# An mLSTM recurrence laid beside projection matmuls: TensorE's order left to a scheduler, or written out as one visit per chunk

## The chip, the core and the metric

The kernel runs on one core of a Trainium2 chip. The metric is the device time of one execution in microseconds (us), and smaller is better. The engines that matter here work in parallel, each through its own list of instructions in a fixed order: PE (TensorE, matmuls and transposes), DVE (VectorE), ACT (ScalarE), POOL (GpSimd) and SP (which issues most DMAs). An engine waits at an instruction whose input isn't there yet, and all that stands behind it on that engine waits too.

## What is computed

The program is one inference step of a two-layer encoder with width 1024, over 1024 prompt rows and 32 rows of a second sequence (1056 in all). Layer 0 mixes the rows by an mLSTM with 4 heads; then come an MLP, a layer with band attention, and another MLP. The change lies in layer 0. Cut to what matters there:

```python
def mlstm_mixer(u, conv_prev, C0, n0, m0, w_in, b_if, conv_w, conv_b, mhn_g, w_out, chunk_len):
    proj = u @ w_in                      # q,k | v | o | gates
    ...
    qk, conv_new = causal_conv(qk_pre, conv_prev, conv_w, conv_b)
    qk = jax.nn.silu(qk)
    ...
    h, C, n, m = mlstm_scan(q, k, vh, ig, lf, C0, n0, m0, chunk_len)
    mu = h.mean(-1, keepdims=True)
    var = jnp.square(h - mu).mean(-1, keepdims=True)
    h = (h - mu) * lax.rsqrt(var + HEAD_NORM_EPS) * mhn_g
    h = h.reshape(Bsz, S, V_A) * jax.nn.sigmoid(o_pre)
    return h @ w_out, conv_new, C, n, m

def mlstm_chunk(carry, xs):              # one chunk of the scan, for each head
    ...
    s = jnp.einsum('bthd,bshd->btsh', q, k) * wts
    num = jnp.einsum('btsh,bshv->bthv', s, v) + a[..., None] * jnp.einsum('bhvd,bthd->bthv', C, q)
    den = s.sum(axis=2) + a * jnp.einsum('bhd,bthd->bth', n, q)
    h = num / jnp.maximum(jnp.abs(den), jnp.exp(-m_t))[..., None]
    ...
    C_new = a_last[..., None, None] * C + jnp.einsum('bsh,bshv,bshd->bhvd', w_s, v, k)
```

The outputs also hold the final states C of each head for both sequences.

## The kernel before, in words

**Projections.** All matrices are multiplied as three matmuls of split operands (high by high, high by low, low by high): `proj` at L118 to L120 for the projections q and k (`qk`, 128 output rows by 384 or 288 columns) and the output gate (`o`), and `v_chunk` at L487 to L489 for v. One group is 24 matmuls into one PSUM tile. The groups of one head are `qk_proj` (two times three column blocks), then `v_proj` (nine row blocks); `o_proj([0, 1])` comes after the last head.

**The recurrence.** The generator `mlstm(h, ...)` walks over the 9 chunks of head h (8 of 128 rows, and the 32 rows of the second sequence). In visit i it does, for chunk i, `scores` (TensorE: the scores `S` at L668, and a transpose of k at L669; DVE multiplies by the weights into `sT`, L671; ACT scales k into `kw`, L677; POOL makes `qc`, L675); for chunk i-1, `values` (TensorE: the numerator `num` at L686 and L688, the state update `cu` at L690; DVE: the new state `ct` at L693 and statistics `st` at L705; ACT copies the numerator into `hn`, L708); for chunk i-2, `state_out` (only chunks 7 and 8: transposes `co`, and a DMA). After every third chunk `scales` runs a chain of small steps on `sm`, 128 by 3 (L715 to L727, DVE but for two steps on ACT), and then ACT normalises the three `hn` (L731). `heads` transposes the normalised chunk (`hT`, L738) and ACT copies it to `G` (L739). `S`, `hT`, the transposed state `clp` (L660, chunk 8) and `co` share two PSUM buffers (the tag `tp`); `num` and `cu` share two others, and the projections have three.

**What sets the order.** `Flow` holds generators, and `flow.tick()` advances each. While head h projects, the recurrence of head h-1 is advanced by one visit after each projection group. A second task, `ada_l0`, is advanced by the same ticks. It computes the conditioning vectors of later stages on DVE: 128 by 512 multiply-adds (L281 and L279, `ada_acc`), transposes and sums (L288, L290), and a few tiny matmuls (`adas`). The calls only give the order in which instructions are written. A scheduler then builds the list of each engine from a priority heap and a cost model, unless an engine is named in `tc.manual_schedule`, where the written order stays. Before the change that is not so here, and the scheduler places the recurrence's matmuls one by one among the projection's.

Of the kernel before, what the change touches and what calls it, by code (L numbers as in the profile page):

```python
# [8 lines left out]
F32 = mybir.dt.float32  # L9
# [6 lines left out]
P = 128  # L16
# [5 lines left out]
NT = T // P + 1  # L22
# [4 lines left out]
NH = 4  # L27
# [48 lines left out]
def trunk_kernel(ctx: ExitStack, tc: tile.TileContext, a, o):  # L76
    nc = tc.nc
    flow = Flow()
# [94 lines left out]
    def mmt(name):  # L173
        return pa.tile([P, 512], F32, tag="mm", name=name, bufs=3)
# [197 lines left out]
    def uap(hl, k, t0, n):  # L372
        off = hl * UF + k * T + t0
        return U[:, off:off + n]
# [12 lines left out]
    A = A_cm.__enter__()  # L387
# [85 lines left out]
    def v_weight(h, half):  # L473
        def srcs(raw):
            r0 = 512 * half
            r = [(raw[:, :, 0:256],
                  w_in[r0:r0 + 512, 1024 + h * 256:1024 + (h + 1) * 256].rearrange("(k p) c -> p k c", p=P))]
            if h == 0:
                r.append((raw[:, :, 256:264], w_in[r0:r0 + 512, 3072:3080].rearrange("(k p) c -> p k c", p=P)))
            return r  # L480
        return wtile(f"v{h}_{half}", srcs, 264 if h == 0 else 256)

    def v_chunk(ps, ws, t, k):
        w = ws[k // 4]
        n = w.shape[-1]
        uh, ul = uap(0, k, t * P, P), uap(1, k, t * P, P)
        nc.tensor.matmul(ps[:, :n], uh, w[:, 0, k % 4, :], start=(k == 0), stop=False)  # L487
        nc.tensor.matmul(ps[:, :n], uh, w[:, 1, k % 4, :], start=False, stop=False)
        nc.tensor.matmul(ps[:, :n], ul, w[:, 0, k % 4, :], start=False, stop=(k == KC - 1))  # L489

    def v_out(ps, h, t):
        m = P if t < NT - 1 else TS
        vt = A.tile([P, 258], F32, tag="vt", name=f"vt_{h}_{t}", bufs=9)
        nc.scalar.copy(vt[:m, :256], ps[:m, :256])
        nc.gpsimd.memset(vt[:m, 256:258], 1.0)
        if h == 0:
            nc.vector.tensor_copy(bass.AP(g64.tensor, g64[:m, t, 0:4].offset, [g64[:m].ap[0], [32, 2], [1, 4]]),
                                  ps[:m, 256:264].rearrange("p (a b) -> p a b", a=2))
        return vt

    def v_proj(h, after):
        ws = [v_weight(h, half) for half in range(2)]
        vts = []
        for t in range(NT):
            ps = mmt(f"v_{h}_{t}")
            for k in range(KC):
                v_chunk(ps, ws, t, k)
            vts.append(v_out(ps, h, t))
            after(t)
        return vts  # L510
# [72 lines left out]
    def qk_proj(h, after):  # L583
        def srcs(r0):
            return lambda raw: [(raw[:, :, j * P:(j + 1) * P],
                                 w_in[r0:r0 + 512, j * 512 + h * P:j * 512 + (h + 1) * P].rearrange(
                                     "(k p) c -> p k c", p=P)) for j in range(2)]
        ws = [wtile(f"qk{h}_{i}", srcs(512 * i)) for i in range(2)]
        out = []
        for j in range(2):  # L590
            f = j * 4 + h
            qkp = (y4_tile if (h, j) == (0, 1) else y_tile)([P, YL], f"qkp_{f}")
            nc.gpsimd.memset(qkp[:, 0:3], 0.0)
            nc.gpsimd.tensor_copy(qkp[:, TP + 3:TP + 6], hist[:, f])
            for t0, n in TBS:
                ps = mmt(f"qk_{f}_{t0}")
                proj(ps[:, :n], n, ws, j, lambda hl, k: uap(hl, k, t0, n))
                for off, m, cnd in segs(t0, n):
                    d = t0 + off + 3 + 3 * cnd
                    nc.scalar.copy(qkp[:, d:d + m], ps[:, off:off + m])  # L600
                if TBS[-1][0] == t0:
                    continue
                after()
            nc.gpsimd.tensor_copy(tails[:, 0:3, f], qkp[:, TP:TP + 3])
            nc.gpsimd.tensor_copy(tails[:, 3:6, f], qkp[:, YL - 3:YL])
            y = A.tile([P, YL], F32, tag="y", name=f"y_{f}", bufs=4)
            N = YL - 3
            nc.vector.tensor_scalar(y[:, :N], qkp[:, 0:N], convw[:, f:f + 1], convb[:, f:f + 1],
                                    op0=ALU.mult, op1=ALU.add)
            for i in range(1, 4):  # L610
                nc.vector.scalar_tensor_tensor(y[:, :N], qkp[:, i:i + N], convw[:, i * 8 + f:i * 8 + f + 1], y[:, :N],
                                               op0=ALU.mult, op1=ALU.add)
            for s0, s1 in ((0, 353), (353, 706), (706, N)):
                tmp = A.tile([P, 384], F32, tag="tmp", name=f"sl_{f}_{s0}", bufs=3)[:, :s1 - s0]
                neglogsig(tmp, y[:, s0:s1])
                nc.scalar.activation(tmp, tmp, AF.Exp)
                nc.vector.scalar_tensor_tensor(y[:, s0:s1], y[:, s0:s1], float(P) ** -0.5 if j == 0 else 1.0, tmp,
                                               op0=ALU.mult, op1=ALU.mult)
            out.append(y)
            after()  # L620
        return out

    def o_proj(hs, after):

        ws = {h: [wblock(f"o{h}_{i}", w_in, 512 * i, 2048 + h * 256) for i in range(2)] for h in hs}
        for t0, n in TBS:
            for h in hs:
                for j in range(2):
                    f = 2 * h + j
                    ps = mmt(f"o_{f}_{t0}")  # L630
                    proj(ps[:, :n], n, ws[h], j, lambda hl, k: uap(hl, k, t0, n))
                    tmp = A.tile([P, 384], F32, tag="tmp", name=f"og_{f}_{t0}", bufs=3)[:, :n]
                    neglogsig(tmp, ps[:, :n])
                    nc.scalar.activation(tmp, tmp, AF.Exp)
                    g = G[:, f, t0:t0 + n]
                    nc.vector.scalar_tensor_tensor(g, g, mhg[:, f:f + 1], tmp, op0=ALU.mult, op1=ALU.mult)
                    after()

    def mlstm(h, qT, kT, vts):
# [93 lines left out]
        def heads(c):  # L733
            L, yo, to = geo(c)
            hn = live.pop(c)
            pth = tpt(f"hT_{h}_{c}")
            for j in range(2):
                nc.tensor.transpose(pth[:, j * P:j * P + L], hn[:L, j * P:(j + 1) * P], ident[:L, :L])  # L738
            nc.scalar.copy(G[:, 2 * h:2 * h + 2, to:to + L], pth[:, :256].rearrange("p (j t) -> p j t", j=2)[:, :, :L])  # L739

        def state_out(c):
            if c >= NCK - 1:
                w = 0 if c == NCK - 1 else 1
                nc.gpsimd.tensor_copy(ncol[:, 4 * w + h:4 * w + h + 1], ct[c][:, 256:257])
                ps = tpt(f"co_{h}_{c}")
                for j in range(2):
                    nc.tensor.transpose(ps[:, j * P:(j + 1) * P], ct[c][:, j * P:(j + 1) * P], ident)
                co = A.tile([P, 256], F32, tag="hn", name=f"co_{h}_{c}", bufs=4)
                nc.scalar.copy(co, ps[:, :256])
                nc.sync.dma_start(o["C_s" if w else "C_p"][0, 0, h].rearrange("(j p) k -> p j k", p=P),  # L750
                                  co.rearrange("p (j k) -> p j k", j=2))

        for i in range(NT + 3):
            if i < NT:
                scores(i)
            if 1 <= i <= NT:
                values(i - 1)
            if 2 <= i < NT + 2:
                state_out(i - 2)
            if i >= 4 and i % 3:  # L760
                for c in (i - 4, i - 3)[:3 - i % 3] if i % 3 == 1 else (i - 3,):
                    heads(c)
            yield

    def tick(*_):
# [36 lines left out]
    vts = [v_first(vw, next_u)]  # L802
# [19 lines left out]
    qk = [qk_proj(0, tick)]  # L822
    flow.finish(gates)
    G = A.tile([P, KC, T], F32, tag="G", name="G")
    ml = None
    for h in range(1, NH):
        unit = [0]

        def after_qk():
            unit[0] += 1  # L830
            if h > 1 or unit[0] >= 3:
                flow.tick()
        if h == 1:
            ml = flow.add(mlstm(0, *qk[0], vts[0]))
        qk.append(qk_proj(h, after_qk))
        vts.append(v_proj(h, tick))
        flow.finish(ml)
        ml = flow.add(mlstm(h, *qk[h], vts[h]))
    o_proj([0, 1], tick)
    flow.finish(ml)  # L840

    def out_rows():
        ps = tpt("tails_ps")
# [740 lines left out]
    mm, norm, _, out_proj, _, add_gated_at = make_layer(acc, bank, uap)  # L1584
# [333 lines left out]
    for gp in range(2):  # L1918
        for i in range(17):
            c = slim[gp][i // 2] if i % 2 else wide[i // 2] if i < 16 else slim[gp][8]  # L1920
            if not gp and i < 2:
                c = 7 + i
# [244 lines left out]
```

## Time and profile before

| what | value |
|---|---|
| median of 3 runs | 2411.29 us (2409.8 to 2412.41) |
| profiled execution, its own time | 2412.41 us |
| its span in the profile | 2410.6 us |
| TensorE busy | 2342.7 us, 97% of the span |
| DVE busy | 1939.0 us, 80% |
| ACT busy | 1206.0 us, 50% |
| mean granted TensorE clock | 0.995 of full speed |

The changed part runs from about 98 us (the projections of the second head, with the recurrence of the first beside it) to about 386 us (the recurrence of the last head beside the output gates). Times in the trace count from the start of the span. The share of busy time is an average over all stages; for the change, the rows of this part decide.

### The profile page before, as it was taken

The page shows a single profiled execution, that of the slowest core. Times are in us where ns is not written, and L with a number is a line of the kernel's source. Part 1 is how long each engine was busy: PE and PEld are TensorE (multiplying, and loading weights), DVE is VectorE, ACT ScalarE, POOL GpSimd, SP SyncE. Part 2 cuts the span into 40 slices and gives each one's busy share as a digit, 9 for nine tenths or more (in the row PEclk, how much of TensorE's full clock was granted, in tenths as well). Part 3 has the DMA queues.
Part 4 walks back from the last instruction along what each step waited for, and adds up shares of the span by engine and source line. Part 5 has one row for each costly group of instructions (what it writes and reads, how often), then busy time and mean ns, then how long its engine had stood idle before and what let it go on. Part 6 is the DMA issues. An engine that isn't in the chain of part 4 may idle for free. (4 is left out here: it accounts for less than half of the span.)

```text
span 2410.6 us, 44188 instructions
## 1 busy us (share of the span) xinstructions
PE 2342.7 (97%) x17180; PEld 2250.4 (93%) x17180; DVE 1939.0 (80%) x3903; ACT 1206.0 (50%) x2454; POOL 168.1 (7%) x320
## 2 busy tenths in 40 slices
PE   7999999999999999999999999999999999899997
PEld 4999999999999999999999987789999999899997
DVE  4888766778788789989888777756998889888778
ACT  4565557278666630101147467773776777222212
POOL 0111100000000000000000224420000000000003
PEclk9999999999999999999999999999999999999999
DMA  8343222526566896675512330051486779976642
GB/s 302 120 131 103 78 89 66 177 91 206 184 198 200 279 336 230 252 261 215 183 56 89 82 93 1 10 140 59 165 278 211 259 278 335 355 256 236 224 146 73
DMA packets 284277, 424.64 MB, mean 176 GB/s; under 512 B 15384, under 2 KB 205228, under 8 KB 278948
## 3 DMA queue, kind: packets, MB, share of 16 engines
q1 hardware_dynamic: 279860, 391.48, 48.3%
q10 hardware_dynamic: 4208, 30.35, 3.1%
q8 instruction: 135, 2.21, 0.4%
q14 instruction: 74, 0.61, 0.1%
HBM read 305.96 MB, written 118.17 MB: 176 GB/s over the span
## 5 line engine op out<-in xcount | busy, mean ns | idle before, releaser
L1082 DVE SCALAR_TENSOR_TENSOR ACX<-dn,ada,ACX 128x264 f32<-128x264 f32 (+6 forms) x664 | 281.8, 447 | 83.2 <-PE dn L1452 41.1
L1452 PE MATMUL dn<-fx,wf_d 128*128 128x264 f32 x2016 | 254.1, 285 | 6.8 <-DVE ACX L1082 3.5
L1452 PEld LDWEIGHTS dn<-fx,wf_d 128*128 128x128 f32 x2016 | 248.8, 188 | 9.0 <-DVE ACX L1082 3.0
L89 ACT CAST w_dn<-raw_dn 128x1024 fp32r<-128x1024 f32 x36 | 37.7, 1050 | 282.1 <-DVE aw L279 136.9
L118 PE MATMUL dn<-hs,w_dn 128*128 128x384 f32 (+2 forms) x512 | 161.2, 315 | 0.0
L119 PE MATMUL dn<-hs,w_dn 128*128 128x384 f32 (+2 forms) x512 | 161.0, 315 | 0.0
L120 PE MATMUL dn<-hs,w_dn 128*128 128x384 f32 (+2 forms) x512 | 156.4, 314 | 1.3 <-DVE w_dn L90 1.3
L1317 PE MATMUL up<-TF,wf_u 128*128 128x264 f32 x1056 | 143.2, 285 | 3.8 <-ACT H L1320 3.8
L1317 PE MATMUL up<-U,wf_u 128*128 128x264 f32 x1056 | 140.3, 285 | 1.7 <-ACT H L1320 1.2
L1317 PE MATMUL up<-u,wf_u 128*128 128x264 f32 x1056 | 139.7, 285 | 1.3 <-ACT wf_u L89 0.7
L279 DVE SCALAR_TENSOR_TENSOR aw<-radw,cs,aw 128x512 f32<-128x512 f32 x196 | 139.5, 743 | 1.1 <-DMA radw<-in_w_ada_dram 1.1
L1317 PEld LDWEIGHTS up<-TF,wf_u 128*128 128x128 f32 x1056 | 134.4, 189 | 4.8 <-ACT H L1320 4.6
L1317 PEld LDWEIGHTS up<-U,wf_u 128*128 128x128 f32 x1056 | 133.0, 188 | 3.0 <-ACT H L1320 1.6
L1317 PEld LDWEIGHTS up<-u,wf_u 128*128 128x128 f32 x1056 | 132.9, 188 | 1.9 <-ACT wf_u L89 0.9
L118 PE MATMUL dn<-U,w_dn 128*128 128x384 f32 (+2 forms) x416 | 129.4, 312 | 0.6 <-DVE ada L304 0.6
L119 PE MATMUL dn<-U,w_dn 128*128 128x384 f32 (+2 forms) x416 | 129.4, 312 | 0.0
L120 PE MATMUL dn<-U,w_dn 128*128 128x384 f32 (+2 forms) x416 | 125.9, 313 | 0.6 <-DVE w_dn L90 0.5
L1817 ACT ACTIVATE p<-p,mx 128x576 f32<-128x576 f32 (+9 forms) x132 | 86.6, 657 | 27.5 <-DVE mx L1814 25.2
L120 PEld LDWEIGHTS dn<-hs,w_dn 128*128 128x128 f32 x512 | 96.0, 188 | 2.0 <-DVE w_dn L90 1.8
L118 PEld LDWEIGHTS dn<-hs,w_dn 128*128 128x128 f32 x512 | 96.5, 189 | 0.1
L119 PEld LDWEIGHTS dn<-hs,w_dn 128*128 128x128 f32 x512 | 96.6, 189 | 0.0
L90 DVE TENSOR_TENSOR HL<-H,HL 128x1056 fp32r<-128x1056 f32 x64 | 80.3, 1254 | 20.0 <-ACT HL L89 19.9
(403 smaller groups left out, 7111.0 us busy)
## 6 DMA issues: line engine op xcount, KB each, us to landing
hpl<-HL SPq DMA_DIRECT2D x144, 264.0 KB
rdn_u<-in_w_up_dram SPq DMA_DIRECT2D x64, 512.0 KB
hd<-HL SPq DMA_DIRECT2D x28, 1056.0 KB
fx<-hd SPq DMA_DIRECT2D x50, 528.0 KB
radw<-in_w_ada_dram SPq DMA_DIRECT2D x24, 1024.0 KB
hd<-HM SPq DMA_DIRECT2D x28, 792.0 KB
raw_up<-in_w_up_dram SPq DMA_DIRECT2D x40, 512.0 KB
raw_dn<-in_w_down_dram SPq DMA_DIRECT2D x36, 512.0 KB
```

The costliest lines, as they stand in the source:

```text
L89: nc.scalar.copy(dst_h, src)
L90: (eng or nc.vector).tensor_sub(dst_l, src, dst_h.bitcast(F32))
L118: nc.tensor.matmul(ps, wh, mov(0, k), start=(k == 0), stop=False)
L119: nc.tensor.matmul(ps, wh, mov(1, k), start=False, stop=False)
L120: nc.tensor.matmul(ps, wl, mov(0, k), start=False, stop=(k == nk - 1))
L279: nc.vector.scalar_tensor_tensor(acc[cnd], raw[:, k], sc, acc[cnd], op0=ALU.mult, op1=ALU.add)
L1082: nc.vector.scalar_tensor_tensor(xs, ps[:, off + o:off + o + mm_], gate[:, fc, cnd:cnd + 1], xs, op0=ALU.mult, op1=ALU.add)
L1317: nc.tensor.matmul(p, self.ws[w][:, wl, k], moving(f, tp, xl, k), start=first and k + n_ == 0, stop=k == 3 and n_ == 2, skip_group_check=n ...
L1452: nc.tensor.matmul(p, ws[w][:, wl, k], t[:, s0, xl], start=first and k + n_ == 0, stop=k == kg - 1 and n_ == 2, skip_group_check=not first)
L1817: nc.scalar.activation(z, z, AF.Exp, bias=mx[:, 0:1], scale=-1.0, accum_out=mx[:, 1:2])
```

## The change

Three edits. The loop over the heads 2 to 4, and `o_proj([0, 1])` with the rest of the recurrence, stand in `tc.manual_schedule` for PE, so TensorE's list there is the written order: one whole projection group, one visit, the next group. In a visit the order is now `heads`, `state_out`, `scores`, `values` (before: `scores`, `values`, `state_out`, `heads`), and `heads` comes one visit later: chunks 0 and 1 in visit 5, 2 in visit 6, 3 and 4 in visit 8, 5 in visit 9, 6 and 7 in visit 11, 8 in visit 12. The tile `co` leaves the four `hn` buffers for the three `tmp` buffers. The lists of the other engines stay with the scheduler.

```diff
-                co = A.tile([P, 256], F32, tag="hn", name=f"co_{h}_{c}", bufs=4)
+                co = A.tile([P, 384], F32, tag="tmp", name=f"co_{h}_{c}", bufs=3)[:, :256]
...
-        for i in range(NT + 3):
+        for i in range(NT + 4):
+            if i >= 5 and i % 3 != 1:
+                for c in (i - 5, i - 4) if i % 3 == 2 else (i - 4,):
+                    heads(c)
+            if 2 <= i < NT + 2:
+                state_out(i - 2)
             if i < NT:
                 scores(i)
             if 1 <= i <= NT:
                 values(i - 1)
-            if 2 <= i < NT + 2:
-                state_out(i - 2)
-            if i >= 4 and i % 3:
-                for c in (i - 4, i - 3)[:3 - i % 3] if i % 3 == 1 else (i - 3,):
-                    heads(c)
             yield
...
-    for h in range(1, NH):
+    with tc.manual_schedule(engines={mybir.EngineType.PE}):
+        for h in range(1, NH):
...
-    o_proj([0, 1], tick)
+        o_proj([0, 1], tick)
         flow.finish(ml)
```

On TensorE, visit 5 of the first head, before. The names are a tile's name, the chunk or column block, and a running number; `v_3` and `v_4` are groups of v of the second head.

```order
L488 MATMUL v_3_1618<-w_v_1_1421,U 128x256
L738 MATMUL hT_0_1485<-ident,hn_0_1262 128x128 x2
L489 MATMUL v_3_1618<-w_v_1_1421,U 128x256
L487 MATMUL v_4_1680<-w_v_0_1416,U 128x256
L738 MATMUL hT_1_1489<-ident,hn_1_1316 128x128 x2
L488 MATMUL v_4_1680<-w_v_0_1416,U 128x256
L489 MATMUL v_4_1680<-w_v_0_1416,U 128x256
L487 MATMUL v_4_1680<-w_v_0_1416,U 128x256
L488 MATMUL v_4_1680<-w_v_0_1416,U 128x256
L668 MATMUL S_5_1523<-y_912,y_1040 128x128
L669 MATMUL S_5_1523<-ident,y_1040 128x128
L738 MATMUL hT_2_1545<-ident,hn_2_1395 128x128 x2
```

The same place after.

```order
L489 MATMUL v_1_1487<-w_v_1_1423,U 128x256
L738 MATMUL hT_0_1515<-ident,hn_0_1264 128x128 x2
L738 MATMUL hT_1_1519<-ident,hn_1_1318 128x128 x2
L668 MATMUL S_5_1525<-y_912,y_1040 128x128
L669 MATMUL S_5_1525<-ident,y_1040 128x128
L686 MATMUL num_4_1534<-vt_4_664,sT_4_1467 128x257
L688 MATMUL num_4_1534<-ct_3_1478,qc_4_1469 128x257
L690 MATMUL cu_4_1537<-vt_4_664,kw_4_1471 128x257
L487 MATMUL v_2_1547<-w_v_0_1418,U 128x256
```

The transposes of chunks 0 and 1 have moved from inside `v_3` and `v_4` up to the end of `v_1`, and the whole visit stands behind them.

On TensorE, the transposes of chunk 3 of the second head (names as above), before:

```order
L488 MATMUL v_4_2610<-w_v_1_2345,U 128x256
L738 MATMUL hT_3_2470<-ident,hn_3_2237 128x128 x2
L489 MATMUL v_4_2610<-w_v_1_2345,U 128x256
L487 MATMUL v_4_2610<-w_v_1_2345,U 128x256
L738 MATMUL hT_4_2474<-ident,hn_4_2331 128x128 x2
```

and after:

```order
L489 MATMUL v_2_2472<-w_v_1_2343,U 128x256
L738 MATMUL hT_3_2504<-ident,hn_3_2239 128x128 x2
L738 MATMUL hT_4_2508<-ident,hn_4_2333 128x128 x2
L660 MATMUL clp_2514<-ident,cl_2512 128x128 x2
L668 MATMUL S_8_2522<-y_1170,y_1350 32x32
L669 MATMUL S_8_2522<-ident,y_1350 32x128
L686 MATMUL num_7_2531<-vt_7_1874,sT_7_2451 128x257
```

They have moved from the second half of `v_4` to the end of `v_2`, past some 40 projection matmuls, and the state's transpose, the last scores and a numerator stand behind them.

On DVE, the end of the first head's first chain of scales (`sm_0`, its last step is L727) and the work around it: `sl` and `y` belong to the second head's q and k, `ada_acc` to the conditioning vectors, `w_qk` to the third head's weights. Before:

```order
L617 SCALAR_TENSOR_TENSOR y_1348<-y_1348,sl_706_1367 128x353
L723 SCALAR_TENSOR_TENSOR sm_0_1258<-sm_0_1258 128x3
L693 SCALAR_TENSOR_TENSOR ct_4_1537<-ct_3_1476,albc,cu_4_1535 128x257
L724 TENSOR_SCALAR sm_0_1258<-sm_0_1258 128x3
L706 BN_AGGR sm_3_1478<-st_4_1539 128x2
L281 TENSOR_SCALAR ada_acc<-ada_room,cs 128x512
L725 TENSOR_TENSOR sm_0_1258<-sm_0_1258 128x3
L281 TENSOR_SCALAR ada_acc<-ada_room,cs 128x512
L726 TENSOR_TENSOR sm_0_1258<-sm_0_1258 128x3
L279 SCALAR_TENSOR_TENSOR ada_acc<-ada_room,cs,ada_acc 128x512
L727 SCALAR_TENSOR_TENSOR sm_0_1258<-sm_0_1258 128x3
```

and after:

```order
L723 SCALAR_TENSOR_TENSOR sm_0_1260<-sm_0_1260 128x3
L279 SCALAR_TENSOR_TENSOR ada_acc<-ada_room,cs,ada_acc 128x512
L617 SCALAR_TENSOR_TENSOR y_1350<-y_1350,sl_706_1369 128x353
L724 TENSOR_SCALAR sm_0_1260<-sm_0_1260 128x3
L279 SCALAR_TENSOR_TENSOR ada_acc<-ada_room,cs,ada_acc 128x512
L725 TENSOR_TENSOR sm_0_1260<-sm_0_1260 128x3
L279 SCALAR_TENSOR_TENSOR ada_acc<-ada_room,cs,ada_acc 128x512
L726 TENSOR_TENSOR sm_0_1260<-sm_0_1260 128x3
L90 TENSOR_TENSOR w_qk_1_1931<-raw_qk_1_1928,w_qk_1_1931 128x1024
L727 SCALAR_TENSOR_TENSOR sm_0_1260<-sm_0_1260 128x3
L671 TENSOR_TENSOR sT_5_1528<-S_5_1525,W_5_1523 128x128
```

In the second piece the state `ct_4` has left the place ahead of L727 (it now comes behind `sT_5`). Between `st_3`, some rows further up in both lists, and L727 now stand two L281, six L279 and the split of `w_qk_1`; before there stood two L281, one L279 and the split of `w_qk_0`, which is now further up.

More of the change, by code (lines that the diff above doesn't have):

```diff
@@ L825, in trunk_kernel, with after_qk @@
     ml = None
-    for h in range(1, NH):
[L827 to L836, printed above, removed]
+    with tc.manual_schedule(engines={mybir.EngineType.PE}):
+        for h in range(1, NH):
+            unit = [0]
+            def after_qk():
+                unit[0] += 1
+                if h > 1 or unit[0] >= 3:
+                    flow.tick()
+            if h == 1:
+                ml = flow.add(mlstm(0, *qk[0], vts[0]))
+            qk.append(qk_proj(h, after_qk))
+            vts.append(v_proj(h, tick))
+            flow.finish(ml)
+            ml = flow.add(mlstm(h, *qk[h], vts[h]))
+        o_proj([0, 1], tick)
         flow.finish(ml)
-        ml = flow.add(mlstm(h, *qk[h], vts[h]))
-    o_proj([0, 1], tick)
-    flow.finish(ml)
     def out_rows():
```

## The prediction

> **What bounds the kernel now.** I read the page's list of engines first, then the stages of the changed part, then who waits there, then the timeline at the places where TensorE's order changes.
>
> ```profile
> span 2410.6 us, 44188 instructions
> PE 2342.7 (97%) x17180; PEld 2250.4 (93%) x17180; DVE 1939.0 (80%) x3903; ACT 1206.0 (50%) x2454; POOL 168.1 (7%) x320
> ...
> core 0: us, PE busy (x) PEld busy (x) DVE busy (x) ACT busy (x) POOL busy (x), PEclk, DMA share, GB/s
> 93.00:140.00 47.00, 46.74 (x290) 45.31 (x288) 44.08 (x80) 31.55 (x87) 8.68 (x24) 0.94 0.23 69
> 140.00:212.00 72.00, 70.70 (x489) 66.18 (x488) 62.59 (x148) 41.22 (x116) 11.24 (x33) 1.00 0.38 119
> 212.00:284.00 72.00, 70.52 (x483) 66.25 (x481) 59.48 (x140) 40.17 (x117) 9.84 (x30) 1.00 0.32 102
> 284.00:386.00 102.00, 100.73 (x647) 93.75 (x646) 65.51 (x178) 58.76 (x155) 8.24 (x23) 1.00 0.30 95
> 386.00:450.00 64.00, 63.80 (x400) 63.28 (x399) 46.00 (x89) 33.94 (x71) 0.00 (x0) 1.00 0.45 150
> ...
> PE hT L738 <- ACT hn L731: 3.5, 4, 1.3
> ```
>
> TensorE bounds the whole and this part: 288.69 of 293 us busy between 93 and 386. DVE stands close behind: 44.08 of 47 us (94%) until 140, 62.59 of 72 (87%) in the next window, then 83% and 64%. Behind the part TensorE has 0.2 us idle in 64, so what it loses before 386 nothing gives back: a lag passes on to the end.
>
> What could be won is small. Idle time is 4.3 us; 3.5 of it is `hT` waiting for L731 (last row). More is lost in stretched spacings. The groups by shape, from 98 to 386 us (first and last of 32 rows; count, busy time and mean):
>
> ```profile
> L487 PE MATMUL v<-w_v,U 128*128 128x256 f32 x216 | 63.4, 294 | 0.0
> ...
> L850 PE MATMUL ncol_ps<-ident,ncol 128*8 128x128 f32 x1 | 0.3, 270 | 0.0
> ```
>
> Adding all 32 counts, each by its undisturbed start-to-start spacing (0.175 us for 384 columns, 0.133 for 288, 0.117 for 256, 0.217 for 257, 0.109 for 128), gives about 274 of the 288 us. So some 14 us is the whole excess; about 2.5 of it belongs to the narrow matmuls of the 32 rows, and some 12 us are waits that the scheduler's order now has.
>
> **What the change moves.** No matmul is added or removed. TensorE's instructions of a visit now stand in one block at the end of a projection group, and TensorE can't go past the first whose input isn't there. For each I compare when TensorE arrives with when the input comes.
>
> *First visit of the first head.* `S_0` moves from inside a `qk` group to ahead of it.
>
> ```profile
> 111.76 0.34 PE L118 MATMUL qk<-U,w_qk 128*128 128x384 f32 x1
> 111.93 0.34 PE L119 MATMUL qk<-U,w_qk 128*128 128x384 f32 x1
> ...
> 114.30 0.95 DVE L617 SCALAR_TENSOR_TENSOR y<-y,sl 128x353 f32<-128x353 f32 x2
> ...
> 114.87 0.49 PE L668 MATMUL S<-y,y 128*128 128x128 f32 x2
> ```
>
> TensorE reaches the new place at 111.76, where that group begins; the input, DVE's L617, still comes at 114.87, since DVE's list is the same up to there. Stall 3.1 us.
>
> *Fifth visit of the first head.* Visits 0 to 4 are 6.4 us of their own matmuls; the five groups between are 2 x 24 x 0.175 + 24 x 0.133 + 2 x 24 x 0.117 = 17.3. Started at 114.9, TensorE stands at `hT_0` at 138.6. Its input goes through DVE:
>
> ```profile
> 135.16 0.42 DVE L705 BATCH_NORM_STATS2 st<-num 128x6 f32<-128x256 f32 x1
> ...
> 135.57 1.21 DVE L90 TENSOR_TENSOR w_qk<-raw_qk,w_qk 128x1024 fp32r<-128x1024 f32 x1
> 136.70 0.95 DVE L462 SCALAR_TENSOR_TENSOR sl<-y,sl 128x353 f32<-128x353 f32 x2
> ...
> 138.77 1.39 DVE L617 SCALAR_TENSOR_TENSOR y<-y,sl 128x353 f32<-128x353 f32 x3
> ...
> 140.78 0.46 DVE L281 TENSOR_SCALAR ada_acc<-ada_room,cs 128x512 f32<-128x512 f32 x1
> ...
> 142.35 0.16 DVE L727 SCALAR_TENSOR_TENSOR sm<-sm 128x3 f32<-128x3 f32 x1
> 142.43 2.74 DVE L279 SCALAR_TENSOR_TENSOR ada_acc<-ada_room,cs,ada_acc 128x512 f32<-128x512 f32 x4
> ...
> 142.55 1.59 ACT L731 ACTIVATE hn<-hn,sm 128x256 f32<-128x256 f32 x3 [0.20 <-DVE sm L727]
> ...
> 143.21 0.44 PE L738 MATMUL hT<-ident,hn 128*128 128x128 f32 x2
> ```
>
> Before, `hT_0` ran at 143.21. In the new list DVE has between `st_3` and L727: two L281 (0.39 each), six L279 (2.74/4 = 0.67 each), three L462 and three L617 (0.45 each), one L90 (1.15) and some nine small steps (0.7): 0.8 + 4.0 + 2.7 + 1.15 + 0.7 = 9.3 us. `st_3` ends at about 137.3: `num_3` is done at 135.6, but DVE comes to it late, out of `y` (L611). So L727 ends at 146.5, and the first of three L731 (1.59/3 = 0.53) at about 147.1. Stall: 147.1 - 138.6 = 8.5 us. Bounds: 4.6 if DVE stays as quick as in the trace (143.2), 9.5 if nothing overlaps.
>
> What stands behind: `S_5`, `num_4` and `cu_4`, and with them DVE's `ct_4`, `st_4`, `sT_5`. `S_5` is the third user of the two `tp` buffers and also waits for the copy of `hT_0`, which on ACT comes behind the other two L731 (1.1 us). How long a copy takes:
>
> ```profile
> 360.55 0.38 PE L738 MATMUL hT<-ident,hn 128*128 128x128 f32 x2
> ...
> 360.97 0.37 ACT L739 COPY G<-hT 128x256 f32<-128x256 f32 x1 [0.17 <-PE hT L738]
> ```
>
> 0.79 us from the transposes' start to the copy's end, while TensorE has 0.22 us of `hT_1` to do: 0.6 us in each fifth visit with an idle ACT, 1.0 here. In each eighth visit `clp` and `S_8` wait for copies in the same way, 0.7 us. For the eighth visit of the first head I take 2.3 with them: 1.0 for `hT_3` itself, whose chain also has an L90 and two L290 in it, and the rest for buffers. Sum for the first head: 3.1 + 8.5 + 1.0 + 2.3 = 14.9 us.
>
> *Second head.* DVE is less behind, because TensorE's stalls let it catch up. At the fifth visit only the buffers wait (0.6). At the eighth, DVE has from `st_5` to L727 one L90, three each of L462 and L617, two L281, six L279 and small steps, 11.6 us; TensorE from `num_5`'s end has two v groups and a visit, 7.7 us. The difference and one L731 (0.53), less the 0.4 of `cu_5` that TensorE also does, with roundings: a stall between 4.0 and 5.2; I take 5.2, and 1.0 for the buffers. In the trace:
>
> ```profile
> 221.62 1.58 ACT L731 ACTIVATE hn<-hn,sm 128x256 f32<-128x256 f32 x3 [0.53 <-DVE sm L727]
> ...
> 222.27 0.44 PE L738 MATMUL hT<-ident,hn 128*128 128x128 f32 x2 [1.25 <-ACT hn L731]
> ```
>
> so already before TensorE waited 1.25 us for this tile, at a place 40 matmuls later; 40 x 0.117 + 1.25 = 5.9 says the same. With 0.4 at visit 11: 7.2 us.
>
> *Third and fourth heads.* No `ada_acc` (4.8 us) in the third's chain: 3.5 us with its buffers. In the fourth a visit has 5.8 us between (an `o` group and itself), DVE is 64% busy, and `adas`, which stood behind the part, comes in: 2.0.
>
> *The rest.* `co` in `tmp` frees `hn` buffers, and `tmp` waits for a DMA of 128 KB instead: nothing, since ACT (58.76 of 102 us) and not TensorE would wait for it; without that cover a fraction of a microsecond, twice a head.
>
> Waits after: 14.9 + 7.2 + 3.5 + 2.0 = 27.6. Waits that go: 12. Net +15.6.
>
> **TensorE's clock.** Long idles have a price of their own here.
>
> ```profile
> 92.02 1.13 PE L577 MATMUL ae_ps<-ident,stk 36*128 36x36 f32 x9 [2.42 <-ACT stk L570]
> ...
> 97.00:98.40 1.40, 1.40 (x7) 1.40 (x7) 1.40 (x3) 0.00 (x0) 0.59 (x2) 0.50 0.99 323
> 98.40:100.00 1.60, 1.60 (x13) 1.60 (x13) 1.60 (x2) 1.05 (x1) 0.00 (x0) 0.99 0.86 295
> ...
> 1259.37 0.69 PE L120 MATMUL q<-U,w_q 128*128 128x384 f32 x1 [2.90 <-DVE w_q L90]
> 1259.85 0.52 PE L118 MATMUL q<-U,w_q 128*128 128x384 f32 x1
> 1260.17 0.52 PE L119 MATMUL q<-U,w_q 128*128 128x384 f32 x1
> ...
> 1259.00:1262.00 3.00, 2.63 (x8) 2.63 (x9) 3.00 (x6) 0.52 (x1) 0.00 (x0) 0.50 0.52 144
> 1262.50:1265.00 2.50, 2.34 (x14) 2.02 (x12) 2.44 (x4) 0.59 (x2) 0.00 (x0) 1.00 0.82 234
> ```
>
> Idles of 2.42 and 2.90 us were followed by a granted clock of 0.50 for 6.4 and about 3 us, with matmuls 0.32 apart where 0.17 is usual (111.76 to 111.93): a loss of 1.5 to 3.2 us each. The new stalls of 3.1, 8.5 and 5.2 are all longer. The first one's slowness lies in front of the 8.5 us stall, which DVE sets, so it is absorbed; the other two cost 1.5 each at least. I take 3.0; bounds 0 and 9.6 (three times 3.2).
>
> [...]
>
> **Sum.** 15.6 + 3.0 = +18.6 on the profiled execution's 2412.41, which lies 1.1 above the median of 2411.29: 2431.0, or 2429.9 against the median. I say 2430.
>
> **Rivals.**
> - *DVE keeps its pace and the clock holds* (slower, but less): `hn_0` at 143.2 and no half clock. 18.6 - 3.9 - 3.0 = +11.7, and with the second head's stall halved (-2.6) +9: 2420. For it: TensorE's stalls give DVE air. Against: six L279 stand ahead of L727 where one stood. Chance 0.25.
> - *Faster*: `heads` one visit later is late enough, and the 12 us of present waits go. 2400. It needs L727 to be done before 138 in the first head and the matching places; the trace had it at 142.35, and the list brings more ahead of it. It decides against me if DVE reaches L727 4 us earlier than in the trace. Chance 0.08.
> - *No change*: the new stalls equal the 12 us removed, about half of my 27.6; 2409 to 2414. Chance 0.07, of which 0.05 falls within 0.2% (4.8 us, about what a measurement of this kernel can tell from no change).
> - *Worse*: each stall delays `st` and `ct`, DVE falls behind again, and three clock drops cost 3.2 each: 15.6 + 9.6 + some 3 = +28, 2440. Chance 0.2.
>
> My forecast keeps 0.4. The range from 2414 to 2441 leaves out the faster case, most of no change, and the worst tail. Slower by over 0.2%: 0.4 + 0.25 + 0.2 and 0.01 of no change, 0.86; same 0.05; faster 0.08 + 0.01.
>
> **What the profile after would show.** If right: idle of PE before `hT` L738, released by ACT L731, grows from 3.5 to over 12 us in the part, with single waits of about 8 us near 139 to 147 and 5 us in the second head's eighth visit; one of about 3 us before the first `S` L668; the granted clock in the window 140 to 212 below 1.00; behind the part nothing changes but the start. Wrong, if `hT` finds its input (no wait over 2 us), if DVE's L727 ends near 142 or earlier, or if the part ends before 386.

## The result and the profile after

The changed kernel takes 2438.31 us (median of 4 runs, 2436.03 to 2441.63) against 2410.55 for the kernel before: a ratio of 1.0119, with a 95% interval of 1.0104 to 1.0134. It is 28 us slower; forecast were +18.6 us, a time of 2430 and a range of 2414 to 2441. The profiled execution took 2441.63 us with a span of 2439.8.

The page and the stages of the changed part, after. The windows follow the part as it moves. A window's columns are its length, the busy time and count of PE, PEld (TensorE's weight loads), DVE, ACT and POOL, the granted clock as a share of full speed, the DMA share and GB/s:

```profile
span 2439.8 us, 44197 instructions
...
PE 2347.5 (96%) x17180; PEld 2252.9 (92%) x17180; DVE 1937.2 (79%) x3903; ACT 1205.4 (49%) x2454; POOL 170.2 (7%) x320
...
93.00:140.00 47.00, 43.36 (x269) 42.28 (x267) 43.49 (x77) 29.88 (x77) 10.09 (x23) 0.93 0.24 72
140.00:222.00 82.00, 70.44 (x464) 64.79 (x465) 59.24 (x142) 39.17 (x114) 10.36 (x30) 0.94 0.30 89
222.00:294.00 72.00, 65.04 (x428) 59.72 (x427) 53.24 (x127) 35.24 (x102) 8.72 (x27) 0.95 0.33 102
294.00:410.00 116.00, 110.02 (x708) 101.54 (x709) 77.91 (x205) 62.51 (x173) 10.97 (x30) 0.97 0.29 90
410.00:474.00 64.00, 64.00 (x397) 63.35 (x398) 46.17 (x83) 39.05 (x85) 0.00 (x0) 1.00 0.50 165
```

TensorE does the same 17180 matmuls. In the first four windows it is now idle for 28.1 of 317 us (4.3 of 293 before), and the granted clock, the number after POOL's, is below 1.00 in all four (before, in the first alone). Behind the part TensorE is as full as before.

Who it waits for there, from 98 to 420 us (line waited for: us in total, times, the longest):

```profile
PE hT L738 <- ACT hn L731: 19.8, 7, 8.3
PE S L668 <- DVE y L617: 3.6, 1, 3.6
PE S L668 <- ACT G L739: 2.4, 4, 1.2
PE clp L660 <- ACT G L739: 1.2, 3, 0.6
PE cu L690 <- ACT sm L709: 0.8, 2, 0.4
```

The four longest of these waits in TensorE's timeline (in brackets the idle time ahead and who ended it), and DVE's and ACT's rows at the second:

```profile
113.42 0.58 PE L668 MATMUL S<-y,y 128*128 128x128 f32 x1 [3.59 <-DVE y L617]
148.23 1.18 PE L738 MATMUL hT<-ident,hn 128*128 128x128 f32 x4 [8.28 <-ACT hn L731]
237.11 1.18 PE L738 MATMUL hT<-ident,hn 128*128 128x128 f32 x4 [5.55 <-ACT hn L731]
368.99 1.18 PE L738 MATMUL hT<-ident,hn 128*128 128x128 f32 x4 [2.69 <-ACT hn L731]
...
138.03 0.42 DVE L705 BATCH_NORM_STATS2 st<-num 128x6 f32<-128x256 f32 x1
...
146.25 1.22 DVE L90 TENSOR_TENSOR w_qk<-raw_qk,w_qk 128x1024 fp32r<-128x1024 f32 x1
147.38 0.16 DVE L727 SCALAR_TENSOR_TENSOR sm<-sm 128x3 f32<-128x3 f32 x1
...
147.58 1.58 ACT L731 ACTIVATE hn<-hn,sm 128x256 f32<-128x256 f32 x3 [3.85 <-DVE sm L727]
```

DVE is busy without a gap from `st_3` at 138.03 to L727 at 147.38; TensorE stands at `hT_0` from 139.95 to 148.23. The length, 8.3 us, is that of the prediction (8.5). The place agrees in part by chance: it was forecast as 138.6 to 147.1, but this execution also began the part 2.1 us earlier (next rows), so that in the part's own time both ends came some 3.3 us later than forecast.

The part itself, by its first and last projection matmul of TensorE, before (first two rows) and after:

```profile
100.16 0.34 PE L118 MATMUL qk<-U,w_qk 128*128 128x384 f32 x1
419.93 0.30 PE L120 MATMUL o<-U,w_o 128*128 128x288 f32 x1
...
98.06 0.34 PE L118 MATMUL qk<-U,w_qk 128*128 128x384 f32 x1
452.39 0.29 PE L120 MATMUL o<-U,w_o 128*128 128x288 f32 x1
```

319.8 us became 354.3: the part lost 34.6 us. The execution started it 2.1 us earlier and made good 3.3 us behind it, so the span grew by 29.2. Since the start differs by some microseconds from run to run, the length of the part, from this first to this last matmul, is the fairest measure below.

### The profile page after: what moved, and what is told of

Same layout as the page of the kernel before. It is cut to its first block, busy times and chain, and to the rows that moved or that the text cites. A ratio compares the mean times of both kernels' runs of the same rounds, so it can differ in the third digit from the quotient of the medians.

```text
span 2439.8 us, 44197 instructions
## 1 busy us (share of the span) xinstructions
PE 2347.5 (96%) x17180; PEld 2252.9 (92%) x17180; DVE 1937.2 (79%) x3903; ACT 1205.4 (49%) x2454; POOL 170.2 (7%) x320
## 5 line engine op out<-in xcount | busy, mean ns | idle before, releaser
L279 DVE SCALAR_TENSOR_TENSOR aw<-radw,cs,aw 128x512 f32<-128x512 f32 x196 | 139.3, 742 | 1.6 <-DMA radw<-in_w_ada_dram 1.6
L1818 ACT ACTIVATE p<-p,mx 128x576 f32<-128x576 f32 (+9 forms) x132 | 86.6, 657 | 27.6 <-DVE mx L1815 25.4
```

The costliest lines, as they stand in the source:

```text
L279: nc.vector.scalar_tensor_tensor(acc[cnd], raw[:, k], sc, acc[cnd], op0=ALU.mult, op1=ALU.add)
L1818: nc.scalar.activation(z, z, AF.Exp, bias=mx[:, 0:1], scale=-1.0, accum_out=mx[:, 1:2])
```

## The experiments

Theory A is that of the prediction: in written order TensorE stands at each transpose or score until DVE and ACT have delivered its input. All kernels are timed against the kernel before on the same chip, in batches on several chips; across batches I compare the differences to it (27.8 us for the changed kernel).

**The two halves of the change.** `e1_manual_only` keeps the written order of TensorE but has the old visits; `e2_visits_only` has the new visits and `co`, and leaves the order to the scheduler.

```diff
 e1: with tc.manual_schedule(engines={PE}): ... (as changed)
-        for i in range(NT + 4):      # heads, state_out, scores, values
+        for i in range(NT + 3):      # scores, values, state_out, heads (as before)
 e2: for i in range(NT + 4): ...      (as changed)
-    with tc.manual_schedule(engines={mybir.EngineType.PE}):
```

> TensorE's written order as in the changed kernel, but each visit as before the change (scores, values, states, heads; heads one visit earlier). Theory A (the cost is TensorE standing at a transpose or a score whose input DVE and ACT deliver later; how late a visit comes decides): the long waits of the changed kernel grow by about one projection group each, 8.3 to about 11 us and 5.5 to about 8, and the last head's 2.7 by up to 5; with the half clock behind them 2448 to 2462 us. Rival B (the cost is the block order itself, with its buffers, whatever the place of heads): 2434 to 2442, as the changed kernel.

> The new order inside a visit, heads one visit later and co in tmp, but the scheduler orders TensorE as before. Theory A: it places the matmuls by when it thinks them ready, so this part alone does nothing: 2406 to 2414 us, no single wait over 2 us beside the projections. Rival C (the later heads or co's new buffer cost by themselves): 2418 us or more.

e2 took 2408.67 us, 1.0001 (0.9992 to 1.0010) of before: no change, as A said; the later heads and `co`'s buffer do nothing where the scheduler places the matmuls. e1 took 2476.67 us, 1.0279 (1.0261 to 1.0298): the forecast of B (the cost lies in the block order itself, wherever heads stand) falls, and A's is passed by 15 us. Its rows of the part:

```profile
PE hT L738 <- ACT hn L731: 43.3, 10, 11.1
PE cu L690 <- ACT sm L709: 4.5, 2, 4.0
PE S L668 <- DVE y L617: 2.9, 1, 2.9
```

The longest wait is 11.1 us, as forecast, but there are ten for `hT`, where I had counted three to grow. So the written order makes the loss, and the new visits, which look like part of the damage, take some 41 us of it back (e1 lies 68.6 us above the kernel before, the changed kernel 27.8). The new visits are later heads and another order within a visit; these two runs don't separate them.

**DVE's other work.** The L279 multiply-adds of the conditioning vectors are left out, in the changed kernel and in the one before.

```diff
                     if half or k:
+                        if base == 16:
+                            continue
                         nc.vector.scalar_tensor_tensor(acc[cnd], raw[:, k], sc, acc[cnd], op0=ALU.mult, op1=ALU.add)
```

> The changed kernel without DVE's multiply-adds L279 of the conditioning vectors that run beside the recurrence (only the first product of each sum is left; the vectors come out as that one product). To be read against the next one. Theory A with DVE as what is late: the waits shrink by the L279 that stood ahead of each input: the first 3.6 to about 1.5, 8.3 to about 4, 5.5 to about 1.5; fewer half-clock stretches; the difference to the same kernel with the scheduler's order falls from 28 us to 8 to 16. Rival B (block order itself, ACT or the PSUM buffers): the difference stays at 24 to 30.

> The kernel before, with the same multiply-adds left out. All theories: TensorE-bound, so little: 2400 to 2411 us, less by at most the waits for hT (3.5 us) and the vector sums later on.

2424.47 and 2409.83 us: a difference of 14.6, inside A's 8 to 16. In the first:

```profile
PE hT L740 <- ACT hn L733: 8.4, 3, 4.0
...
PE S L670 <- DVE y L619: 2.9, 1, 2.9
```

(L740 is L738 here, two lines were added.) The wait of 8.3 us is now 4.0, which is shorter by about the six L279 of 0.67 that stood in its way; that of 5.55 is 3.3, where I had said 1.5; the first is 2.9, not 1.5. So about half of the loss, 13 of 28 us, is this one kind of other work of DVE, ahead of what TensorE stands for. The other half remains without it.

**Later visits.** `e7_s0_later` starts the first head's recurrence a group later; `e8_heads_later` has heads two more visits later; `e9_all_later` has both, and the vector steps further apart.

```diff
 e7, e9:
-                if h > 1 or unit[0] >= 3:
+                if h > 1 or unit[0] >= 4:
 e8, e9:
-            if i >= 5 and i % 3 != 1:
-                for c in (i - 5, i - 4) if i % 3 == 2 else (i - 4,):
+            if i >= 7 and i % 3:
+                for c in (i - 7, i - 6) if i % 3 == 1 else (i - 6,):
                     heads(c)             # hn: 6 buffers, tmp and W: 2 each
 e9:
-    ADA_C = (2.0, 3.0, 2.0)
+    ADA_C = (3.0, 4.0, 3.0)
```

> The changed kernel, with the first head's recurrence starting one projection group later (4.2 us). Theory A: the 3.6 us wait before the first S goes, with its half clock, and hT_0's wait of 8.3 stays or shrinks by as much as DVE gets ahead in the 4.2 us: 2428 to 2435 us. Rival (the later waits are set by DVE alone, so that what is won at S is paid at hT_0): 2436 to 2440.

> The changed kernel with heads two visits later still (chunks 0 and 1 in visit 7, 2 in 8, 3 and 4 in 10, and so on), six hn buffers in place of four, and for the room two tmp and two W buffers in place of three. Theory A (lateness of hn decides): the waits for hT go (19.8 us in the changed kernel) with three of four half-clock stretches (8.2 us); the first S keeps 3.6 and 2.9: 2410 to 2417 us. Rival B (what is late is DVE as a whole, and waits move to the scores and numerators or the buffers): 2425 to 2440.

> As the one before, and the recurrence of the first head one group later, and the conditioning vectors' steps 1.4 times as far apart. A candidate to beat both kernels. Theory A: no wait over 1 us is left in the part, and up to 10 us of the scheduler's own waits go: 2398 to 2408 us. Rival B: as the one before or worse.

e7: 2430.69 us (1.0090, 1.0075 to 1.0106), as A said. The first wait is gone, `hT_0`'s is 3.0 instead of 8.3, a new one of 3.1 stands at `cu`, and the second head's wait for `hT` grew from 5.55 to 6.5. e8: 2417.15 (1.0039, 1.0026 to 1.0052), 0.15 us above A's range. The waits for L731 are gone altogether, and others are left:

```profile
PE co L747 <- ACT G L739: 4.8, 4, 2.1
PE S L668 <- ACT G L739: 4.6, 7, 2.2
PE S L668 <- DVE y L617: 3.7, 1, 3.7
```

e8 lies 9.6 us above the kernel before, so lateness of `hn`, with the half clock that followed it, is some 18 of the 28 us. (e8 also has other numbers of buffers, for room.) What it leaves is the first `S`'s wait, and waits for the two buffers that `S`, `hT`, `clp` and `co` share: they come free when ACT has copied `G`. e9: 2416.15 (1.0035, 1.0022 to 1.0048), not below 2408 as A had it. The first `S` no longer waits, but the buffers' rows are as large (5.5 and 4.3 us).

**The buffers.** Two ways out of them, and one that keeps the old pace of the vectors.

```diff
 e10 (from e9): scores, values, state_out, heads, with heads one visit earlier:
+            if i >= 6 and i % 3 != 2:
+                for c in (i - 6, i - 5) if i % 3 == 0 else (i - 5,):
+                    heads(c)
 e11 (from e9), e13 (from e8 with the later first S):
-        return pa.tile([P, 512], F32, tag="tp", name=name, bufs=2)
+        return pa.tile([P, 512], F32, tag="tp", name=name, bufs=3)
-        return pa.tile([P, 512], F32, tag="ada", name=name, bufs=1)
+        return pa.tile([P, 512], F32, tag="nm", name=name, bufs=2)
```

> As e9 (late heads, first S later, vector steps further apart), but heads stand last in a visit, one visit earlier, so that a whole projection group lies between the copies of hT and the next user of their two buffers. In e9 TensorE still waits 5.5 us at S and 4.3 us at co for those copies. Theory A with the buffers as its second part: these 9.8 us go: 2404 to 2410 us. Rival D (the copies wait behind other work of ACT in any order, or the visits as blocks cost elsewhere): 2413 to 2418.

> As e9, with three PSUM buffers for S, hT, clp and co in place of two (the sums of the conditioning vectors move to the buffers of num and cu). Theory A with the buffers: 2405 to 2411 us. Rival D: 2413 to 2418.

> As e11 (heads two visits later, first S a group later, three buffers for S, hT, clp and co), with the vector steps at their old pace, since in e11 the slower pace put their loads ahead of the next stage's weights on the DMA queue (TensorE then waited 3.4 and 9.1 us for w_oa). In e11 the part itself, from the second head's v to the last output gate, took 288.3 us against 292.7 in the kernel before. Theory A with the buffers: no wait over 2.5 us, part as in e11 or a little longer, 2401 to 2408 us, at or below the kernel before. Rival D (block order costs as much as the scheduler's): 2410 or more.

e10: 2415.07 us (1.0025, 1.0016 to 1.0035), rival D's time. The waits at `S` and `co` went, but `hT` now waits for the buffers instead (8.2 us in three rows, the longest 3.4). e11: 2447.88 (1.0163, 1.0150 to 1.0177), far off both. In the part the waits fall as A said, to 5.0 us; it is behind the part that it loses, 36 us (2027.2 us from the part's last matmul to the end, against 1990.7). TensorE's rows from 420 to 460 us:

```profile
PE op_a L118 <- ACT w_oa L89: 12.5, 2, 9.1
PE adas L301 <- DVE cx L290: 1.5, 1, 1.5
```

The weights of the next stage come late: two of their loads are issued right behind loads for the vectors (438.4 behind 437.5, 448.9 behind 447.8), and the vectors' last sum begins at 484.5 us, against 428.4 in e9. The slower pace alone doesn't do this: e9 has it too, and loses nothing behind the part. What e11 adds to e9 are the buffers, with the vectors' sums moved among them; how that makes them late isn't shown. The part itself tells what three buffers are worth. Its first and last matmul (e11, then e13):

```profile
102.58 0.34 PE L118 MATMUL qk<-U,w_qk 128*128 128x384 f32 x1
419.99 0.30 PE L120 MATMUL o<-U,w_o 128*128 128x288 f32 x1
...
99.36 0.34 PE L118 MATMUL qk<-U,w_qk 128*128 128x384 f32 x1
421.47 0.29 PE L120 MATMUL o<-U,w_o 128*128 128x288 f32 x1
```

With the later visits and three buffers the part ends where it did before (419.93), though e11 began it 2.4 us later: it is 317.4 us long, 2.4 us less than the 319.8 of the scheduler's order, and 11.7 less than e9's 329.1. So in the part itself a written order need not cost anything, once each block stands late enough and has the buffers. e13, with the old pace, took 2428.73 us (1.0081, 1.0067 to 1.0095), a miss. Its part is 322.1 us long; behind it TensorE stands 3.8 us at the next weights and 8.4 us at `adas`, whose input comes from DVE at 448.8 us. In the kernel before the same `adas` waited 0.2 us: there 153 matmuls of the next stage stood ahead of it in TensorE's list, here 72. What three buffers win in the part is lost behind it, in both kernels. No version beat the kernel before.

**The clock.** Matmuls that nobody reads stand ahead of the long waits and keep TensorE busy in them.

```diff
+            fill = {(0, 0): 15, (0, 5): 40, (1, 8): 25, (3, 5): 10}.get((h, i), 0)
+            if fill:
+                fp = mmt(f"fill_{h}_{i}")
+                for r in range(fill):
+                    nc.tensor.matmul(fp[:, :384], uap(0, 0, 0, P), uap(0, 1, 0, 384), start=True, stop=True)
```

> The changed kernel with matmuls that nobody reads (128 by 384, 0.175 us each) ahead of the four long waits: 15 before the first S, 40 before hT_0 of the first head, 25 before hT_3 of the second, 10 before hT_0 of the fourth, each a little shorter than the wait, so that TensorE keeps working while DVE and ACT deliver. It tells the clock from the waits. If the half clock follows TensorE's idleness and its four stretches cost what their working time says (2.9 + 2.6 + 2.5 + 3.1 us): 2427 to 2431 us, with no half clock between 100 and 400 us. If the first stretch is hidden in the 8.3 us wait, as the prediction had it: 2429 to 2432. If the clock hardly matters: 2436 to 2440.

> The changed kernel again with unread matmuls ahead of its long waits, more of them (18, 51, 31, 9 and 13), so that no idle time over 1 us is left at these places. e6 kept three half-clock stretches of 3.4 us and ended the part 2 us before the changed kernel. To be read from the time at which the part ends, since the later stages of these kernels differ by up to 5 us with the same lists. If the clock's loss is TensorE's own (5.1 to 8 us left to win): the part ends 5 us or more before the changed kernel's. If DVE and ACT set the pace in these stretches, so that a faster TensorE only waits longer: it ends within 3 us of it. The whole: 2432 to 2447 us.

e6 took 2445.83 us (1.0159, 1.0145 to 1.0173), slower than the changed kernel and outside all three forecasts. Its part still had three half-clock stretches of 3.4 us and ended 2.3 us earlier (450.06); it lost 5.1 us in later stages, most of it between 1970 and 2100 us, in lists that are the same as the changed kernel's. I can't say why, so for the clock only the part is read. e12 took 2436.74 (1.0113, 1.0099 to 1.0126). Its part keeps one half-clock stretch of 3.4 us (164.3 to 167.7 us, granted clock 0.51), and ends at:

```profile
447.33 0.29 PE L120 MATMUL o<-U,w_o 128*128 128x288 f32 x1
```

5.1 us before the changed kernel's 452.39, and 5.5 us earlier in the part's own time (it began at 98.51). By the working time in half-clock stretches some 9 us were there to be won (below). The rest became waiting: the unread matmuls are busy for 22.2 us and 9.1 us of idle time are left, 31 us together, where the changed kernel was idle for 27.5. So somewhat over half of the clock's loss was TensorE's own, and in the rest DVE and ACT set the pace. The answer came at the edge between the two forecasts.

## Why the prediction was right, and which terms were off

*The waits: right, place by place.* Idle times over 0.3 us in the changed kernel's part, against the terms of the sum:

| place | predicted | measured |
|---|---|---|
| first head, first `S` | 3.1 | 3.6 |
| first head, `hT_0` | 8.5 | 8.3 |
| first head, the rest | 3.3 | 0.3 + 0.6 + 1.4 |
| second head | 7.2 | 0.9 + 0.4 + 5.55 + 0.4 |
| third head | 3.5 | 1.2 + 0.4 + 1.2 + 0.3 |
| fourth head | 2.0 | 2.7 + 0.3 |
| sum | 27.6 | 27.5 |

The sum is closer than its terms, which are off by up to 1.0 us either way and cancel. The method that gave them was to place TensorE by counting matmuls at their spacing, and DVE by adding the durations of the rows that stand ahead of the input in its new list.

*The clock: mis-sized.* The prediction took 3.0 us and bounded it at 9.6. The stretches at 0.50 in the changed kernel's part last 6.8, 10.2, 6.8 and 6.8 us. TensorE worked in 22 of these 30.6 us, so by this estimate (half of the 22, at half speed) its matmuls took 11 us longer. The step that failed has three parts. The first wait's slowness, 2.9 us, was to be absorbed by the 8.3 us wait, as if DVE alone set its end. But DVE's rows ahead of it begin with `st_3`, which needs TensorE's `num_3`. In e12, which lacks that stretch, `st_3` comes 22.1 us after the first `S` (24.6 in the changed kernel) and `hT_0` 33.3 us after it (34.8): 1.0 us was absorbed and 1.5 came through. The two drops that I counted cost some 2.5 us each, not 1.5. And I didn't count the 2.7 us wait of the fourth head as one that drops the clock (some 3 us).

*The waits that go: mis-sized.* All 12 us were to go. By the same count of spacings the changed part has 49.4 us over its undisturbed length: 27.5 of idle times, 11 of clock and 10.9 in small pieces, against 14.9 before. Of the 14.9, 3.5 were idle rows, and these did go; the small pieces were 11.4 before and are 10.9 now. Less the 2.5 of the narrow matmuls, about 8 of the 12 us are still there. So the step that failed is that all stretched spacings were put down to the scheduler's order, when only 3.5 us had a row that showed it. What makes the small pieces isn't shown. Together: 18.6 + 8 for the clock + 8 for this = 34.6, which is what the part lost.

*What made up for it, by luck.* Outside the part 5.4 us came back, 2.1 before and 3.3 behind it; the prediction had nothing there. The kernel before was profiled with half-clock stretches at 91.6 and 1259 us, which the changed kernel's execution didn't have. They explain the 2.1 and some 1.7 of the 3.3 (3.4 us at half speed); the other 1.6 stay open. The mechanism, the places and the lengths of the waits were foreseen. That the time lies inside the range is in part luck: the clock and the waits that go were off by 16 us together, and the 34.6 us that the part lost would on 2410.55 have been 2445, above it.

*The rivals.* That DVE keeps its pace and the clock holds was wrong on both counts. The worse case (+28, 2440) was nearer in time than my 2430; its main part, the clock's 9.6 us, came about (11), its other part, a DVE that falls behind again, did not, since the waits add up to the 27.5 of the table. The faster case needed L727 before 138 us; it ended at 147.5.

## What to carry to other kernels

An order written by hand on the busiest engine is only as good as the place of each instruction against the clock of the engines that feed it: before fixing it, add up, for each instruction that could stall, the rows that stand ahead of its input on the other engine, and put it that much later. A block that waits holds back all that stands behind it, also what was ready (the 8.3 us at `hT_0` held back the group `v_2`, which reads `w_v` and `U` as the group ahead had done), and shared buffers can become waits when their users stand next to each other (4.8 and 4.6 us in e8). Where these two were mended, the written order was no slower in its part (317.4 us in e11, against 319.8), but the loss turned up behind it (36 us in e11): time the part and what follows it apart. Idle time on TensorE cost more than its length here, where half clock came with it: 27.5 us of idle time and, by the estimate above, 11 us of slower matmuls.

## What the runs showed of the hardware

The granted clock in the part of the changed kernel was 0.50 from 112.40 to 119.23 us, from 143.12 to 153.36, from 235.28 to 242.11 and from 368.40 to 375.23, and full between these stretches. The four longest waits, of 3.59, 8.28, 5.55 and 2.69 us, ended at 113.42, 148.23, 237.11 and 368.99 us, each inside one of the stretches. In the first, matmuls of 384 columns stand 0.32 us apart, and behind it 0.175. The rows around the first and the fourth wait, two rows near 91 us of the changed kernel and then of the one before (each row: window, length, busy time of PE, PEld, DVE, ACT and POOL, granted clock, DMA share, GB/s), and TensorE's wait near 91 us in the changed kernel:

```profile
108.99:112.40 3.41, 0.83 (x7) 0.60 (x5) 3.41 (x6) 3.41 (x10) 0.21 (x1) 1.00 0.32 75
112.40:115.81 3.41, 2.40 (x8) 2.40 (x9) 3.41 (x6) 2.88 (x7) 0.51 (x1) 0.50 0.29 83
115.81:119.23 3.42, 3.42 (x12) 3.42 (x12) 3.42 (x5) 0.77 (x2) 0.00 (x0) 0.50 0.00 0
119.23:122.64 3.41, 3.41 (x21) 3.30 (x21) 0.90 (x4) 3.19 (x8) 0.30 (x3) 1.00 0.00 0
...
364.99:368.40 3.41, 1.31 (x8) 0.99 (x6) 3.41 (x14) 1.22 (x5) 0.00 (x0) 1.00 0.00 0
368.40:371.81 3.41, 2.67 (x16) 1.93 (x17) 2.60 (x10) 3.25 (x8) 0.12 (x1) 0.50 0.19 25
...
88.51:91.92 3.41, 1.80 (x11) 1.48 (x9) 3.41 (x5) 0.63 (x2) 0.09 (x1) 1.00 0.02 4
91.92:95.33 3.41, 2.60 (x21) 2.55 (x22) 3.32 (x8) 2.46 (x4) 0.88 (x2) 1.00 0.04 9
...
88.20:91.61 3.41, 1.39 (x8) 1.08 (x7) 3.41 (x4) 1.03 (x2) 0.00 (x0) 1.00 0.03 5
91.61:95.02 3.41, 3.00 (x15) 2.90 (x16) 2.92 (x8) 1.81 (x3) 0.88 (x2) 0.50 0.03 7
...
92.72 0.69 PE L577 MATMUL ae_ps<-ident,stk 36*128 36x36 f32 x8 [2.42 <-ACT stk L570]
```

Ahead of the two half-clock stretches shown TensorE was busy for 0.83 and 1.31 us of 3.41. Near 91 us both kernels' TensorE waited 2.42 us for ACT's `stk` (L570). In the profile of before the granted clock was then 0.50, from 91.61 to 98.43 us; in the one after it stayed at 1.00. So a wait of 2.42 us came with 6.8 us at half clock in one profile and with none in the other, and one of 2.69 us with 6.8: from these the length of a wait alone doesn't tell what it costs beyond itself. What decides isn't shown.
